# A hybrid recurrence block: 18 weight blocks keep their lower parts in DRAM, and dense steps change places

## The chip, the cores and the metric

The kernel runs on one core of a Trainium2 chip. The metric is the device time of one execution in microseconds. Three executions of the kernel before took 2312.27, 2316.17 and 2316.66 us; their median is 2316.17 us. A fourth execution was profiled; it took 2310.18 us itself, and all lines of the profile belong to it.

An engine has its own queue of instructions and works them off in order: TensorE (PE) multiplies matrices, VectorE (DVE), ScalarE (ACT) and GpSimd (POOL) work on elements, and SyncE (SP) issues the DMA transfers between DRAM and the on-chip memory.

## The reference

One residual block over 1024 tokens of width 1024, in float32. The input is normalised and modulated by a condition `c` (six segments of 1024 values, `mod`), and one projection `w_in` feeds two token mixers and two gates:

```python
mod = (cond @ w_ada[l] + b_ada[l])[:, None, :]
u = layer_norm(x) * (1.0 + sc1) + sh1
proj = u @ w_in
q, f, i, g, z, xbc, dt, gate_a, gate_b = jnp.split(proj, offs, axis=-1)
y_a = hgrn2_mixer(q, f, i, g, lb, gnorm) @ w_branch_a
y_b = mamba2_mixer(z, xbc, dt, conv_w, conv_b, dt_bias, a_log, d_skip, ssm_norm) @ w_branch_b
merged = jax.nn.sigmoid(gate_a) * y_a + jax.nn.sigmoid(gate_b) * y_b
x = layer_norm(ALPHA * x + g1 * (merged @ w_o), ln1_g[l], ln1_b[l])
u = layer_norm(x) * (1.0 + sc2) + sh2
x = layer_norm(ALPHA * x + g2 * swiglu(u, ...), ln2_g[l], ln2_b[l])
```

The first mixer (HGRN2) has 8 heads, each a gated linear recurrence with a 128 x 128 state. The second (Mamba-2) has 4 groups of 8 heads; its inputs x, B and C pass a causal convolution of four taps and a silu, and its output is gated by z and normalised per group. Both are computed in chunks over the tokens.

## The kernel before, in words

**Products.** A float32 product is made of three matmuls in a rounded format: each operand is split into an upper part (a cast) and a lower part (operand minus upper part), and lower x upper, upper x lower and upper x upper are added in PSUM (`Dense.mm`, L81 to L83). A weight block is 128 x 1024 (512 KB). `Dense.load` (L65 to L77) loads it into a buffer `raw`, casts it on ACT into `wh` (L75), and subtracts on the engine `dn.lo` to get `wl` (L76). There are two buffers each for `raw`, `wh` and `wl`. `Dense.unit` multiplies one block with both halves of 512 tokens: 8 steps of 3 matmuls for each half, and after each half a function evacuates the PSUM bank.

**Stages.** In time order:

1. 0 to 361 us: modulation, then products that are formed in pairs of blocks with fewer multiplications (gate A, g, z). Among the first pairs stand halves of plain gate blocks.
2. 361 to 467 us, the `i` stage (L558 to L594): the projection `i` and dt, three groups of 352 columns (`iwh`, `iwl`, four raw pieces `iraw` for each group, which use the `raw` buffers too), eight row tiles each. A row tile is 24 matmuls of 352 columns, evacuated on ACT into `i_sb` (L587). Beside it `mods`, a generator, loads blocks `wa` of `w_ada` and adds them up on DVE (L217), for the modulation segments that are needed later; it is advanced after each row tile. `step_sizes` computes Mamba's decays.
3. 467 to about 790 us, `hgrn_phase`: dense units for f and q of each head (lower parts on POOL), with the score, output and state products of the chunks between them.
4. About 790 to 1263 us, `mamba_phase`: dense units for B, C and four x blocks of each group (`dense_x`), followed by the rest of gate B; between them the chunks of the groups (transposes `trx` L871, scores `cb`, `yx` L910, `yi` L918). Lower parts are made on POOL here too.
5. To 1500 us the branch maps (`dqs`), to 1680 us the output projection and norm, then the FFN.

**What sets the order.** In stages 3 and 4 the dense units hang in one chain of generators, `Fill`, and `fill.to(n)` advances it until n steps are done. A step is three matmuls of 512 columns. `HF0` is the number of steps ahead of the first head's preparation, `HF1` the number ahead of its first scores; `share(i)` gives the steps done by chunk i. In mamba, `96 + LEAD` steps stand ahead of the first chunk, 12 go with each chunk of the first three groups, and what is left of `total` is spread over the last group's eight chunks; `LATE` steps remain behind them. `NGB` is the number of gate B blocks done before mamba. A scheduling layer then fixes the order of each engine's queue within these bounds. All transfers are issued by SP, in one order.

Of the kernel before, what the change touches and what calls it, by code (L numbers as in the profile page):

```python
# [9 lines left out]
F32 = mybir.dt.float32  # L10
# [3 lines left out]
ALU = mybir.AluOpType  # L14
PSUM = bass.MemoryType.PSUM

HF0, HF1 = 40, 52
F0, F1 = 0, 3
LATE, LEAD = 32, 12
NGB = 2  # L20
NE0, XJ = 1, 3
NG = 8
IE, MO = "VVVV", 4
# [9 lines left out]
P = 128  # L33
T = 1024
TT = T // P
# [3 lines left out]
HA = 8  # L39
# [11 lines left out]

B_Q, B_F, B_G, B_Z, B_X, B_B, B_C, B_GA, B_GB = 0, 8, 16, 24, 40, 56, 60, 64, 72
NBLK = 80

C_CT, C_BADA, C_CW, C_CB, C_DS, C_NW, C_GN, C_LB = 0, 8, 56, 152, 176, 192, 208, 209
NCOL = 225
# [4 lines left out]
class Dense:  # L61
# [2 lines left out]
    def __init__(self, tc, pool, psum):  # L64
        self.nc, self.pool, self.psum, self.lo = tc.nc, pool, psum, tc.nc.vector  # L65

    def load(self, src, scale=None, into=None, eng=None):
        nc = self.nc
        raw = self.pool.tile([P, 1024], F32, tag="raw", name="raw")
        nc.sync.dma_start(out=raw, in_=src)  # L70
        if scale is not None:
            r2 = raw.rearrange("p (k n) -> p k n", k=2)
            nc.vector.tensor_tensor(r2, r2, scale[:, None, :].broadcast_to([P, 2, TH]), op=ALU.mult)
        wh, wl = into or [self.pool.tile([P, 1024], F32R, tag=t, name=t) for t in ("wh", "wl")]
        nc.scalar.copy(wh, raw)  # L75
        (eng or self.lo).tensor_tensor(wl, raw, wh.bitcast(F32), op=ALU.subtract)  # L76
        return wh, wl  # L77

# [4 lines left out]
        nc.tensor.matmul(ps, sh, mh, start=False, stop=last)  # L83

    def unit(self, src, uh, ul, evac, ths=(0, 1), fine=False):
        wh, wl = src if isinstance(src, (tuple, list)) else self.load(src)
        wh = wh.rearrange("p (k n) -> p k n", k=KT)
        wl = wl.rearrange("p (k n) -> p k n", k=KT)
        for th in ths:
            ps = self.psum.tile([P, TH], F32, tag="d", name="dps")  # L90
            for kt in range(KT):
                self.mm(ps, wh[:, kt, :], wl[:, kt, :], uh[th][:, kt, :], ul[th][:, kt, :],
                        kt == 0, kt == KT - 1)
                if fine and kt < KT - 1:
                    yield
            evac(th, ps)
            yield
# [18 lines left out]
def chain(*gens):  # L116
    for g in gens:
        yield from g
# [3 lines left out]
def hybrid_block(ctx, tc, x, w_mod, w_ada, w_blk, w_i, w_ba, w_bb, w_o, w_g, w_u, w_d,  # L122
                 cols, masks, rows, hrows, out):
    nc = tc.nc
# [25 lines left out]
    z_d = tc.dram_tile([16, P, T], F32, name="z_d")  # L150
    h_d = tc.dram_tile([NFT, P, T], F32, name="h_d")
    x1_d = tc.dram_tile([TT, P, D], F32, name="x1_d")

    mk = const.tile([P, NMASK, P], F32, name="mk")
    cl = const.tile([P, NCOL], F32, name="cl")
# [84 lines left out]
    def gate_evac(which, n, logs=False):  # L240
        dst = (ga_d, gb_d)[which]

        def evac(th, ps):
            sg = wp.tile([P, TH], F32, tag="ge", name="ge")
            if logs:
                act(sg, ps, AF.Exp, scale=-1.0)
                act(sg, sg, AF.Ln, bias=ones[:, 0:1])
                act(sg, sg, AF.Exp, scale=-1.0)
            else:
                act(sg, ps, AF.Sigmoid)  # L250
            nc.sync.dma_start(out=dst[n, :, TH * th:TH * th + TH], in_=sg)
        return evac

    def gate_units(which, n0, n1, fine=False, ths=(0, 1)):
        for n in range(n0, n1):
            yield from dn.unit(w_blk[(B_GA, B_GB)[which] + n], uh, ul, gate_evac(which, n, fine), ths, fine=fine)
# [16 lines left out]
    with tc.tile_pool(name="sw", bufs=1) as sw, tc.tile_pool(name="s0p", bufs=2, space=PSUM) as pp:  # L273
# [149 lines left out]
        for k in range(4):  # L423
            modulate(1, k)
            modulate(1, 4 + k)
            u0, u1 = xT[1][:, k, :], xT[1][:, 4 + k, :]
            c = wp.tile([P, TH], F32, tag="ge", name="ge")
            V.tensor_tensor(c, u1, u0, op=ALU.subtract)
            split(t3[0][:, k, :], t3[1][:, k, :], c, V)
            V.tensor_tensor(u0, u0, b11[0][:, k, :].bitcast(F32), op=ALU.subtract)  # L430
            V.tensor_tensor(u0, u0, b11[1][:, k, :].bitcast(F32), op=ALU.subtract)
            split(t1[0][:, k, :], t1[1][:, k, :], u0, V)
            V.tensor_tensor(u1, u1, u0, op=ALU.subtract)
            split(t2[0][:, k, :], t2[1][:, k, :], u1, V)
            V.tensor_tensor(u0, b21[0][:, k, :].bitcast(F32), u1, op=ALU.subtract)
            V.tensor_tensor(u0, u0, b21[1][:, k, :].bitcast(F32), op=ALU.add)
            split(t4[0][:, k, :], t4[1][:, k, :], u0, V)
            if ns < NF:
                early(ns, *load_a(pairs[ns][0]))
                ns += 1  # L440
            if k % 2:
                n = 6 + k // 2
                for _ in dn.unit(dn.load(w_blk[B_GA + n]), uh, ul, gate_evac(0, n), (0,)):
                    pass
        while ns < NF:
            early(ns, *load_a(pairs[ns][0]))
            ns += 1
# [108 lines left out]
    with tc.tile_pool(name="s1", bufs=2, reuse_waits="tile") as sp, \  # L556
# [6 lines left out]
        def load_i(g, k4):  # L563
            raw = wp.tile([P, 1024], F32, tag="raw", name="iraw")[:, 0:2 * NI].rearrange("p (k n) -> p k n", k=2)
            nc.sync.dma_start(out=raw, in_=w_i[g, :, 2 * k4:2 * k4 + 2, :])
            return raw

        bridge = dn.load(w_blk[B_GA + 6])
        iraw = [load_i(0, k4) for k4 in range(2)]
        for g in range(3):  # L570
            wh = sp.tile([P, KT, NI], F32R, tag="iwh", name="iwh")
            wl = sp.tile([P, KT, NI], F32R, tag="iwl", name="iwl")
            for k4 in range(4):
                ks = slice(2 * k4, 2 * k4 + 2)
                raw = iraw.pop(0) if iraw else load_i(g, k4)
                split(wh[:, ks, :], wl[:, ks, :], raw, V if IE[k4] == "V" else G)
            if g == 0:
                for _ in dn.unit(bridge, uh, ul, gate_evac(0, 6), (1,)):
                    pass
                lower_bound()  # L580
            for tt in range(TT):
                ps = psd.tile([P, TH], F32, tag="d", name="dps")
                th, o = tt // 4, P * (tt % 4)
                for kt in range(KT):
                    dn.mm(ps[:, 0:NI], uh[th][:, kt, o:o + P], ul[th][:, kt, o:o + P], wh[:, kt, :], wl[:, kt, :],
                          kt == 0, kt == KT - 1)
                S.copy(i_sb[:, tt, NI * g:NI * g + NI], ps[:, 0:NI])  # L587
                mods.to((TT * g + tt + 1 - MO) * 36 / (24 - MO))
                if g == 1 and tt == 4:
                    steps.drain()  # L590
            if g == 0:
                steps = Fill(step_sizes(sp, pp))
                steps.to(1)
        mods.drain()  # L594


    def hgrn_phase():
        with tc.tile_pool(name="h", bufs=2, reuse_waits="tile") as hp, \
# [162 lines left out]
                nc.sync.dma_start(out=ya_d[h, :, TH * hf:TH * hf + TH], in_=y)  # L761

            units = [dense_fq(h) for h in range(HA)]
            fill = Fill(chain(*units, gate_units(0, 7, 8, True, (1,)), gate_units(1, 0, NGB, True)))
            fill.to(HF0)
            for g in (prep(0), arrays(0, 0)):
                for _ in g:
                    pass
            fill.to(HF1)
            score(0, 0)  # L770
            total = 16 * (2 * HA + NGB) + 8

            def share(i):

# [31 lines left out]
    def mamba_phase():  # L806
        with tc.tile_pool(name="m", bufs=2, reuse_waits="tile") as mp, \
# [3 lines left out]
            def dense_x(g):  # L811
# [6 lines left out]
                for blk, dst in [(16 + g, bT), (20 + g, cT)] + [(4 * g + j, xT[:, j, :]) for j in range(4)]:  # L818
# [22 lines left out]
                                act(t, t, AF.Silu, bias=cl[:, C_CB + k:C_CB + k + 1])  # L841
                            held[:] = held[1:] if len(held) == 2 and not th else []

                    yield from dn.unit(w_blk[B_X + blk], uh, ul, evac, fine=True)

            def fetch(g, ch):

# [620 lines left out]
```

## Time and profile before

| | |
|---|---|
| median of three runs | 2316.17 us |
| profiled execution, its own time | 2310.18 us |
| its span in the trace | 2308.4 us |
| TensorE busy | 2230.2 us, 97% |
| VectorE, ScalarE, GpSimd busy | 1567.8, 1061.6, 264.8 us |
| mean DMA rate over the span | 126 GB/s |

The trace names instructions by line and tile. A wait is listed with the instruction that released it, and a window gives each engine's busy time, the clock that TensorE was granted as a share of full speed, the share of time that the 16 DMA engines were busy, and the rate that they moved. A gap on TensorE costs time; a gap on another engine does only if something waits for it.

### The profile page before, as it was taken

The page shows a single profiled execution, that of the slowest core. Times are in us where ns is not written, and L with a number is a line of the kernel's source. Part 1 is how long each engine was busy: PE and PEld are TensorE (multiplying, and loading weights), DVE is VectorE, ACT ScalarE, POOL GpSimd, SP SyncE. Part 2 cuts the span into 40 slices and gives each one's busy share as a digit, 9 for nine tenths or more (in the row PEclk, how much of TensorE's full clock was granted, in tenths as well). Part 3 has the DMA queues.
Part 4 walks back from the last instruction along what each step waited for, and adds up shares of the span by engine and source line. Part 5 has one row for each costly group of instructions (what it writes and reads, how often), then busy time and mean ns, then how long its engine had stood idle before and what let it go on. Part 6 is the DMA issues. An engine that isn't in the chain of part 4 may idle for free.

```text
span 2308.4 us, 32125 instructions
## 1 busy us (share of the span) xinstructions
PE 2230.2 (97%) x12412; PEld 1816.2 (79%) x12412; DVE 1567.8 (68%) x2489; ACT 1061.6 (46%) x1931; POOL 264.8 (11%) x153
## 2 busy tenths in 40 slices
PE   7899999999999999999998999999899999999998
PEld 4778889977777787787776788888788888888886
DVE  5866665638898558898975443468977666653647
ACT  3833333137777646777786320224633333322221
POOL 0000000012222222222231000003400000000000
PEclk9999999999999999999999999999999999999999
DMA  7334326601112312343455643432232222244554
GB/s 282 121 140 136 126 93 209 218 33 52 61 56 69 118 61 92 110 141 115 159 164 183 229 167 102 132 138 95 73 132 101 87 73 92 73 160 151 179 182 132
DMA packets 119649, 290.75 MB, mean 126 GB/s; under 512 B 12101, under 2 KB 26949, under 8 KB 119497
## 3 DMA queue, kind: packets, MB, share of 16 engines
q1 hardware_dynamic: 119496, 288.71, 37.5%
q8 instruction: 97, 1.59, 0.3%
q14 instruction: 56, 0.45, 0.1%
HBM read 235.05 MB, written 53.62 MB: 125 GB/s over the span
## 4 chain that ended last, share of the span: by engine, by line
PE 82%; DVE 8%; ACT 3%; issue 3%; DMA 2%; POOL 2%; SPq 0%; DVEq 0%; POOLq 0%; ACTq 0%
PE dps L81 11%; PE dps L83 11%; PE dps L82 11%; PE fps L81 9%; PE fps L82 9%; PE fps L83 9%; PE dqs L81 4%; PE dqs L83 4%; PE dqs L82 4%; PE hps L83 1%; PE hps L81 1%; PE hps L82 1%; PE sc_ps L701 1%; DVE xTm L832 1%; PE yi L918 1%
## 5 line engine op out<-in xcount | busy, mean ns | idle before, releaser
L81 PE MATMUL dps<-uh,wl 128*128 128x512 f32 x800 | 331.7, 415 | 3.3 <-POOL wl L76 3.3
L83 PE MATMUL dps<-uh,wh 128*128 128x512 f32 x800 | 316.5, 396 | 0.0
L82 PE MATMUL dps<-ul,wh 128*128 128x512 f32 x800 | 314.8, 393 | 0.0
L76 POOL TENSOR_TENSOR wl<-raw,wh 128x1024 fp32r<-128x1024 f32 x49 | 132.1, 2696 | 790.4 <-ACT wh L75 723.4
L81 PEld LDWEIGHTS dps<-uh,wl 128*128 128x128 f32 x800 | 155.1, 194 | 37.6 <-issue 6.6
L83 PEld LDWEIGHTS dps<-uh,wh 128*128 128x128 f32 x800 | 151.9, 190 | 33.8
L82 PEld LDWEIGHTS dps<-ul,wh 128*128 128x128 f32 x800 | 152.5, 191 | 26.7
L81 PE MATMUL dqs<-yp,wl 128*128 128x512 f32 x384 | 147.5, 393 | 6.6 <-ACT yp L191 4.3
L82 PE MATMUL dqs<-yp,wh 128*128 128x512 f32 x384 | 150.4, 392 | 0.0
L83 PE MATMUL dqs<-yp,wh 128*128 128x512 f32 x384 | 150.1, 391 | 0.0
L179 POOL TENSOR_TENSOR mv<-mv,kc 128x1 f32<-128x1 f32 x32 | 32.3, 1015 | 1026.7 <-DVE mv L178 1023.5
L191 ACT CAST cw<-raw 128x512 fp32r<-128x512 f32 x131 | 81.0, 621 | 132.3 <-PE fps L83 87.6
L81 PE MATMUL fps<-t,cw 128*128 128x512 f32 x352 | 137.0, 389 | 0.7 <-DVE cw L192 0.7
L82 PE MATMUL fps<-t,cw 128*128 128x512 f32 x352 | 136.9, 389 | 0.0
L83 PE MATMUL fps<-t,cw 128*128 128x512 f32 x352 | 136.9, 389 | 0.0
L75 ACT CAST wh<-raw 128x1024 fp32r<-128x1024 f32 x76 | 79.6, 1048 | 113.5 <-PE dqs L83 101.8
L192 DVE TENSOR_TENSOR cw<-raw,cw 128x512 fp32r<-128x512 f32 x131 | 94.8, 725 | 43.5 <-ACT cw L191 42.2
L82 PE MATMUL fps<-wl,hp 128*128 128x512 f32 x304 | 118.4, 389 | 0.0
L83 PE MATMUL fps<-wh,hp 128*128 128x512 f32 x304 | 118.3, 389 | 0.0
L192 DVE TENSOR_TENSOR wl<-wdr,wh 128x1024 fp32r<-128x1024 f32 x38 | 46.5, 1224 | 105.4 <-ACT wh L191 105.2
L81 PE MATMUL fps<-wh,hp 128*128 128x512 f32 x304 | 117.0, 390 | 0.5 <-ACT wh L191 0.5
L191 ACT CAST wh<-wdr 128x1024 fp32r<-128x1024 f32 x38 | 40.1, 1054 | 147.4 <-PE fps L83 146.1
(368 smaller groups left out, 5586.4 us busy)
## 6 DMA issues: line engine op xcount, KB each, us to landing
raw<-in_w_blk_dram SPq DMA_DIRECT2D x79, 512.0 KB, 3.4
wdr<-in_w_d_dram SPq DMA_DIRECT2D x44, 512.0 KB, 3.8
wa<-in_w_ada_dram SPq DMA_DIRECT2D x32, 512.0 KB, 4.5
ac<-ac_d SPq DMA_DIRECT2D x32, 512.0 KB, 4.8
raw<-in_w_g_dram SPq DMA_DIRECT2D x26, 512.0 KB, 3.8
raw<-in_w_u_dram SPq DMA_DIRECT2D x26, 512.0 KB, 3.5
hr<-h_d SPq DMA_DIRECT2D x44, 256.0 KB, 3.9
h_d<-sg SPq DMA_DIRECT2D x18, 512.0 KB, 2.9
```

The source lines that it names most:

```text
L75: nc.scalar.copy(wh, raw)
L76: (eng or self.lo).tensor_tensor(wl, raw, wh.bitcast(F32), op=ALU.subtract)
L81: nc.tensor.matmul(ps, sl, mh, start=first, stop=False)
L82: nc.tensor.matmul(ps, sh, ml, start=False, stop=False)
L83: nc.tensor.matmul(ps, sh, mh, start=False, stop=last)
L179: G.tensor_tensor(mv[:, 2:3], mv[:, 1:2], kc[:, 2:3], op=ALU.pow)
L191: S.copy(hi, src)
L192: eng.tensor_tensor(lo, src, hi.bitcast(F32), op=ALU.subtract)
L701: PE.matmul(sp_[b0:b1, 0, b1:b2], lv[c][:, o + b0:o + b1], lv[c][:, o + b1:o + b2], start=True, stop=True)
L832: V.scalar_tensor_tensor(d[:, o:], ps[:, o + j - 3:TH + j - 3], cw(j), d[:, o:], op0=ALU.mult, op1=ALU.add)
L918: PE.matmul(yi[64 * e:64 * e + 64, j, :], xd[:, HP * hh:HP * hh + HP], ac[:, hh, :], start=True, stop=True)
```

## The change

It has three parts.

**Lower parts in DRAM.** The blocks of B, C and x of mamba's groups 1 to 3 (18 blocks, `AHEAD`) are loaded in the `i` stage, cast, subtracted on DVE, and the lower parts written to a DRAM tensor `wl_d`. This is a second generator, `make_lower`, which is advanced after each row tile beside `mods`. In mamba, these blocks are loaded and cast again, and their lower part is loaded from `wl_d` instead of being subtracted on POOL.

**Half gate blocks.** The first halves of gate B's blocks 0 and 1 move to the first pairs, next to the halves of gate A's blocks 6 and 7; their second halves, and all of block 2, are done in `hgrn_phase`, whose number of steps stays 296. The chain in mamba loses 16 steps.

**Counts.** HF0, HF1 go from 40, 52 to 32, 60; LEAD from 12 to 16. So the last group has 4 steps a chunk instead of 6.5, and the last 12 chunks of `hgrn_phase` have 2.33 instead of 3.

```diff
-HF0, HF1 = 40, 52
+HF0, HF1 = 32, 60
-LATE, LEAD = 32, 12
-NGB = 2
+LATE, LEAD = 32, 16
+NGB = 3
...
+AHEAD = [b for g in range(1, 4) for b in [B_B + g, B_C + g] + [B_X + 4 * g + j for j in range(4)]]
...
-    def load(self, src, scale=None, into=None, eng=None):
+    def load(self, src, scale=None, into=None, eng=None, lower=None):
...
         nc.scalar.copy(wh, raw)
+        if lower is not None:
+            nc.sync.dma_start(out=wl.bitcast(F32), in_=lower)
+            return wh, wl
         (eng or self.lo).tensor_tensor(wl, raw, wh.bitcast(F32), op=ALU.subtract)
...
-        wh, wl = src if isinstance(src, (tuple, list)) else self.load(src)
+        wh, wl = src() if callable(src) else src if isinstance(src, (tuple, list)) else self.load(src)
...
+    wl_d = tc.dram_tile([len(AHEAD), P, 1024], F32, name="wl_d")
...
+    made = {}
+    def weights(blk):
+        return (lambda: dn.load(w_blk[blk], lower=wl_d[made[blk]])) if blk in made else w_blk[blk]
+    def make_lower(blks):
+        last = None
+        for blk in blks + [None]:
+            wl = dn.load(w_blk[blk])[1] if blk is not None else None
+            if last:
+                made[last[0]] = len(made)
+                nc.sync.dma_start(out=wl_d[made[last[0]]], in_=last[1].bitcast(F32))
+            last = blk, wl
+            yield
...
             if k % 2:
-                n = 6 + k // 2
-                for _ in dn.unit(dn.load(w_blk[B_GA + n]), uh, ul, gate_evac(0, n), (0,)):
-                    pass
+                for which, n in ((0, 6 + k // 2), (1, k // 2)):
+                    for _ in gate_units(which, n, n + 1, ths=(0,)):
+                        pass
...
+        lower = Fill(make_lower(AHEAD))
...
                 mods.to((TT * g + tt + 1 - MO) * 36 / (24 - MO))
+                lower.to((TT * g + tt) * (len(AHEAD) + 1) / 22)
...
         mods.drain()
+        lower.drain()
...
-            fill = Fill(chain(*units, gate_units(0, 7, 8, True, (1,)), gate_units(1, 0, NGB, True)))
+            fill = Fill(chain(*units, gate_units(0, 7, 8, True, (1,)), gate_units(1, 0, 2, True, (1,)), gate_units(1, 2, NGB, True)))
...
-            total = 16 * (2 * HA + NGB) + 8
+            total = 16 * (2 * HA + NGB) - 8
...
-                    yield from dn.unit(w_blk[B_X + blk], uh, ul, evac, fine=True)
+                    yield from dn.unit(weights(B_X + blk), uh, ul, evac, fine=True)
```

The queues show what this does to the order. First ScalarE's queue in the `i` stage, from the third row tile of group 0 on in the kernel before (`i_sb` is a row tile's evacuation, `iwh` a cast of the next group's weights):

```order
L587 COPY i_sb<-dps 128x352 x3
L191 CAST iwh<-iraw 128x704
L587 COPY i_sb<-dps 128x352
L191 CAST iwh<-iraw 128x704
L587 COPY i_sb<-dps 128x352
L191 CAST iwh<-iraw 128x704 x2
```

and from the fourth row tile on in the changed one (`wh` is the cast of one of the 18 blocks):

```order
L610 COPY i_sb<-dps 128x352
L76 CAST wh<-raw 128x1024
L610 COPY i_sb<-dps 128x352 x2
L76 CAST wh<-raw 128x1024 x2
L610 COPY i_sb<-dps 128x352 x2
L76 CAST wh<-raw 128x1024
L141 ACTIVATE adt<-adt 128x256
L141 ACTIVATE hr<-hr 128x32
L196 CAST iwh<-iraw 128x704 x4
```

The four casts of group 1's weights stood between the third and the sixth evacuation; now all four stand behind the eighth, the seventh block's cast and two activations of `step_sizes`.

SP's queue at the same place, before, from the loads that follow group 0's last raw pieces:

```order
L213 DMA wa<-in_w_ada_dram 128x1024
L251 DMA ga_d<-ge 128x512
L213 DMA wa<-in_w_ada_dram 128x1024 x2
L516 DMA hr<-in_hrows_dram 128x64
L213 DMA wa<-in_w_ada_dram 128x1024 x4
L565 DMA iraw<-in_w_i_dram 128x704 x2
```

and now, the end of the same piece (`raw` are the 18 blocks, `wl_d` their lower parts on the way out):

```order
L272 DMA wl_d<-wl 128x1024
L218 DMA wa<-in_w_ada_dram 128x1024
L71 DMA raw<-in_w_blk_dram 128x1024
L272 DMA wl_d<-wl 128x1024
L538 DMA hr<-in_hrows_dram 128x64
L587 DMA iraw<-in_w_i_dram 128x704
L218 DMA wa<-in_w_ada_dram 128x1024
L587 DMA iraw<-in_w_i_dram 128x704
```

Group 1's first piece stood behind seven `wa` loads; now seven blocks and six written lower parts stand ahead of it as well.

Last, ScalarE's queue at the start of `hgrn_phase`, before (`ab<-dps` are evacuations of head 0's f, q and of the next head's f; `ab<-ab,mk` is the first instruction of head 0's preparation):

```order
L137 ACTIVATE ab<-dps 128x512 x2
L75 CAST wh<-raw 128x1024
L137 ACTIVATE ab<-dps 128x512
L617 COPY xq<-dps 128x512
L137 ACTIVATE ab<-dps 128x512
L617 COPY xq<-dps 128x512
L75 CAST wh<-raw 128x1024
L137 ACTIVATE ab<-dps 128x512
L137 ACTIVATE ab<-ab,mk 128x1024
```

and now:

```order
L141 ACTIVATE ab<-dps 128x512 x2
L76 CAST wh<-raw 128x1024
L141 ACTIVATE ab<-dps 128x512
L642 COPY xq<-dps 128x512
L141 ACTIVATE ab<-dps 128x512
L642 COPY xq<-dps 128x512
L141 ACTIVATE ab<-ab,mk 128x1024
L76 CAST wh<-raw 128x1024
```

The preparation stood behind the fifth evacuation; now it follows the fourth.

## The prediction

> **What bounds the kernel now.** I read the page's first two parts, the stretches of the `i` projection, and then what TensorE waited for in the later phases.
>
> ```profile
> span 2308.4 us, 32125 instructions
> PE 2230.2 (97%) x12412; PEld 1816.2 (79%) x12412; DVE 1567.8 (68%) x2489; ACT 1061.6 (46%) x1931; POOL 264.8 (11%) x153
> 1800.00:1900.00 100.00, 100.00 (x443) 82.81 (x442) 65.26 (x102) 31.80 (x53) 0.00 (x0) 1.00 0.23 79
> ```
>
> TensorE (PE) is busy for 97% of the span, so a matmul that moves without closing a gap changes nothing, and about 78 us of gaps (2308.4 − 2230.2), with the slower clock behind them, are all there is to win. The third row is a stretch of 100 us full of 512-column matmuls: 443 of them, 225.7 ns each. That is my price for a dense matmul; a dense *step* is three of them, 0.677 us.
>
> The stage in which the change adds most is the `i` projection, between about 361 and 467 us. The columns are: window, its length, busy time and count of PE, weight load, DVE, ACT and POOL, granted clock, DMA share, GB/s.
>
> ```profile
> 360.00:380.00 20.00, 19.89 (x121) 19.33 (x120) 13.50 (x20) 7.22 (x12) 0.00 (x0) 1.00 0.95 331
> 420.00:440.00 20.00, 20.00 (x133) 20.00 (x132) 10.50 (x11) 1.81 (x4) 0.00 (x0) 1.00 0.80 271
> 440.00:460.00 20.00, 20.00 (x119) 18.23 (x119) 11.02 (x10) 2.27 (x5) 0.00 (x0) 1.00 0.54 181
> DMA packets 7073, 22.51 MB, mean 212 GB/s; under 512 B 909, under 2 KB 1165, under 8 KB 7066
> iraw<-in_w_i_dram SPq DMA_DIRECT2D x8, 352.0 KB, 3.9
> raw<-in_w_blk_dram SPq DMA_DIRECT2D x4, 512.0 KB, 4.3
> ```
>
> PE waits for nothing here, ACT is nearly idle, DVE is half busy; the DMA engines are the resource closest to full, at 0.54 to 0.95 of their time. The last three rows are the transfers of 361 to 467 us: 22.51 MB in all, and a weight piece lands about 4 us after its issue.
>
> **The change part by part.**
>
> *Half gates among the pairs.* Two half blocks of gate B, 24 matmuls each, move there: 48 × 225.7 ns = **+10.8**. TensorE has no idle time in this stretch that they could fill (its two gaps of 4 us each are chains that start at a product standing behind them), so all of it is paid here and taken off in the last mamba group.
>
> *Eighteen lower parts made in the `i` stage.* Each adds a load, a cast on ACT, a subtraction on DVE and a write, in a stage whose durations are these:
>
> ```profile
> L217 DVE SCALAR_TENSOR_TENSOR acc<-wa,cond,acc 128x1024 f32<-128x1024 f32 x28 | 38.1, 1359 | 11.6 <-DMA wa<-in_w_ada_dram 11.4
> L192 DVE TENSOR_TENSOR iwl<-iraw,iwh 128x704 fp32r<-128x704 f32 x10 | 8.8, 889 | 7.5 <-ACT iwh L191 7.5
> L191 ACT CAST iwh<-iraw 128x704 fp32r<-128x704 f32 x9 | 7.0, 784 | 7.6 <-DMA iraw<-in_w_i_dram 7.6
> L76 POOL TENSOR_TENSOR wl<-raw,wh 128x1024 fp32r<-128x1024 f32 x2 | 5.2, 2608 | 350.1 <-ACT wh L75 350.1
> 461.40 0.45 ACT L587 COPY i_sb<-dps 128x352 f32<-128x352 f32 x1 [3.36 <-PE dps L83]
> 465.22 0.45 ACT L587 COPY i_sb<-dps 128x352 f32<-128x352 f32 x1 [3.36 <-PE dps L83]
> 1263.90 1.04 ACT L75 CAST wh<-raw 128x1024 fp32r<-128x1024 f32 x1
> 1264.96 1.23 DVE L76 TENSOR_TENSOR wl<-raw,wh 128x1024 fp32r<-128x1024 f32 x1 [6.12 <-ACT wh L75]
> ```
>
> ACT gains 18 × 1.04 = 19 us and DVE 18 × 1.23 = 22 us, which both have room for. What they have no room for is their place in the queues. The order (front part) shows the casts of the next group's weights, `iwh`, before the last row tiles of group 0 in the kernel before, and behind all eight copies, a `wh` cast and two small activations in the changed one. SP's queue stands likewise: the four pieces `iraw` come after seven blocks, six writes and seven `wa` loads, and every piece shares the two `raw` buffers with the blocks. Let 0 be the end of group 0's matmuls. Copy 0.45, cast 1.04 and subtraction 1.23 end at 2.7; only then is the buffer free that the second piece is loaded into. It lands at 6.6 (3.9 after its issue), is cast and subtracted (0.78 + 0.89) by 8.3, and frees the buffer of the fourth piece, which lands at 12.2 and is ready at 13.9. TensorE's order mixes three row tiles, so it works meanwhile; but some 26 of their 72 matmuls stand behind the first that needs the fourth piece. One tile of 24 takes 465.22 − 461.40 = 3.82 us, so the three are done at 13.9 + 4.1 = 18.0 instead of 11.5: 6.5 us late. The same order stands between groups 1 and 2. With 1 us each for the clock that drops after a wait (priced at the mamba rows below), that is 2 × 7.5 = 15. At the end, F0's raw block, which in the kernel before is loaded long ahead, now stands behind the last writes and loads; group 2 has some 24 transfers of about 1.6 us (0.52 MB at 331 GB/s), 38 us, against 8 × 3.82 + 6.5 = 37.1 us of matmuls and wait, and then cast 1.04 and POOL's 2.61 follow: about 5 us late. Sum **+20**. A second way to it: 22.51 MB and 36 transfers of 0.524 MB are 41.4 MB, which at the 331 GB/s of the full window take 125 us instead of the 106 there are: +19. Lower bound 0 (every load lands early and PE never waits; nothing waits now, so there is no gain); upper bound +34, if the volume's 19 and one boundary's wait come on top of each other with casts that hold up the copies, and so PSUM, in group 0 as well.
>
> The Trainium skill (DMA: Bandwidth & Descriptors, "Specifications" and "Bandwidth") puts the ceiling of the DMA fabric at 435 GB/s and measures about 425 GB/s for one core alone with 16 MB. By that, the 41.4 MB would take 97 us, the stage would not be bound by volume, and only the waits at the boundaries would be left of this term. The trace has half-microsecond slices above 400 GB/s between 360 and 380 us, but the mean there is 331 GB/s at a share of 0.95, and I keep the row.
>
> *Start of the recurrence.* Here the rows are:
>
> ```profile
> PE sc_ps L701 <- DVE e L676: 3.3, 1, 3.3
> PE sc_ps L705 <- DVE e L676: 3.2, 1, 3.2
> 510.00:520.00 10.00, 10.00 (x80) 6.94 (x79) 7.17 (x14) 6.07 (x15) 0.00 (x0) 0.74 0.01 2
> 489.01 0.60 ACT L137 ACTIVATE ab<-dps 128x512 f32<-128x512 f32 x1 [4.36 <-PE dps L83]
> 494.45 0.60 ACT L137 ACTIVATE ab<-dps 128x512 f32<-128x512 f32 x1 [3.42 <-PE dps L83]
> 494.94 1.14 ACT L137 ACTIVATE ab<-ab,mk 128x1024 f32<-128x1024 f32 x1
> 502.90 3.42 DVE L649 TENSOR_TENSOR ab<-b,ab 128x1024 f32<-128x1024 f32 x1
> ```
>
> PE waits 3.3 us at 505 and 3.2 at 544, and runs at 0.74 for 10 us after the first (2.6 lost). With HF0 at 32 the preparation of head 0 starts behind the evacuation at 489.0 and the copy, not behind that of 494.45: about 4.8 us earlier, less one cast (1.04) that now stands inside its chain. The subtraction on POOL that slows L649 to 3.42 falls elsewhere. But 168 dense matmuls stand before the first score in both orders, and in the new one all 16 score matmuls of a tile come at once, which need the last of the preparation. I expect the first wait to stay near 3, the second and half the lost clock to go: 3.2 + 1.3 + about 1.5 of clock after the second, **−6**. Bounds: −11 (both waits, the 2.6, and as much again after the second) and +4 (a full wait for the later part of the chain in place of 6 matmuls between). The last twelve chunks of this phase lose 8 dense matmuls of cover in all (2.33 steps a chunk, not 3, made up elsewhere): **+1**.
>
> *Mamba groups 0 to 2.*
>
> ```profile
> PE dps L81 <- POOL wl L76: 2.4, 1, 2.4
> PE dps L81 <- POOL wl L76: 1.0, 1, 1.0
> PE trx L871 <- ACT xTm L137: 4.0, 1, 4.0
> PE trx L871 <- ACT xTm L137: 3.4, 1, 3.4
> 1050.00:1060.00 10.00, 8.65 (x48) 7.26 (x49) 7.49 (x16) 7.60 (x18) 0.02 (x1) 0.83 0.39 107
> 1150.00:1160.00 10.00, 7.21 (x32) 5.91 (x32) 7.96 (x17) 6.90 (x18) 1.27 (x1) 0.83 0.39 130
> ```
>
> The first two waits are for lower parts from POOL, which these groups no longer make: −3.4. The two at the start of a group are for the last silu; LEAD 16 puts 4 more steps, 2.7 us, ahead of the transposes: −5.4. Behind each of the two stands a window at 0.83, some 1.4 us of clock (0.17 × 8.65), most of which goes: −2.2. Sum **−11**, bounds −14 (all four waits and both clocks) and −5 (the silus come late as before, behind casts that are still on ACT, and only the lower parts are won).
>
> *Last group and its end.*
>
> ```profile
> 1163.30:1213.30 50.00, 50.00 (x315) 38.76 (x314) 39.58 (x58) 42.71 (x103) 19.35 (x10) 1.00 0.59 184
> PE dqs L81 <- ACT yp L191: 4.3, 1, 4.3
> PE yi L918 <- ACT csh L191: 3.2, 1, 3.2
> ```
>
> 16 steps fewer are 48 × 225.7 ns, −10.8, if they are all on the path. A chunk keeps 4 dense steps of 6.5, so PE's part of its 8.3 us falls by 1.7 to 6.6; but DVE works 39.58/50 and ACT 42.71/50 of that, 6.6 and 7.1 us a chunk, of which ACT gives up only the gate activations that left. I take 7.05 a chunk: 8 × (8.35 − 7.05) = −10.4 of the −13.5 of these chunks; LEAD's 12 matmuls are paid ahead, +2.7. Behind the last sum stand 27 dense matmuls, not 42, so the wait for `yp` (4.3 now) grows by 15 × 0.2257 = 3.4. Sum −10.4 + 2.7 + 3.4 = **−4**, bounds −10.8 and +2 (chunks stay near 8).
>
> **Sum:** 10.8 + 20 − 6 + 1 − 11 − 4 = +10.8. The profiled execution took 2310.18 us, so it becomes 2321; the median of the three runs shown stands 6.0 above it, at 2316.17, and becomes **2327**.
>
> **Rivals.** (a) *The `i` stage absorbs its new work.* Its term is 0, the rest stays: −9.2, **2307**, faster. For it speak the idle ACT and DVE and a mean of 212 GB/s; the rate of the skill's page points the same way. Against it, the casts behind the eighth copy, an order that no early load can mend. (b) *DMA and SP's order decide the whole stage.* Each late block holds up ACT's copies and so PE already in group 0; the term is +34 and the sum +25, **2341**, slower. It decides from the point where 41.4 MB do not fit into the stage and its waits, 106 + 14 us, at under 345 GB/s; 331 speaks for it, against it that early pieces overlap. (c) *The waits removed are worth their upper bounds*: −11 at the recurrence, −14 and −10.8 in mamba, the rest standing: 10.8 + 20 − 11 + 1 − 14 − 10.8 = −4, **2312**, no change that can be told. For it, the clock rows show that a wait costs more than its length; against it, the busy DVE and ACT of the last group.
>
> **How the numbers follow.** A run of this kernel can be told from no change by about 0.2%, 4.6 us. My forecast gets 0.48, (b) 0.15, (a) 0.19, (c) 0.18. The forecast's own spread, ±7, lies nearly all above 2320.8. Slower 0.61, within 0.2% 0.18, faster 0.21. The range runs from 2304, a little under (a), to 2342, at (b); all low ends together (2292) and all high ones (2363) are outside.
>
> **What would show it.** In the new profile: PE gaps of some 6 us in all near the 8th and 16th row tile of the `i` stage, released by `iwl` or `iwh`, and one before F0 released by `wl` of POOL or the load; about 41 MB in that stage and its length near 126 us. No `wl` of POOL in groups 1 to 3, waits for `xTm` under 1.5 us. Last-group chunks of 7 us and a wait for `yp` of 7 to 8 us. An `i` stage of about 106 us would make the prediction wrong on its largest term, chunks at 6.6 or 8 us on the last.

## The result, and the profile after

The changed kernel takes 2339.17 us (median of four runs, 2333.9 to 2342.39), the kernel before 2316.24 us beside it (median of four). The ratio is 1.0101, with a 95% interval of 1.0076 to 1.0126: slower by 0.8 to 1.3%. The profiled execution took 2333.9 us, against 2310.18 before.

The page's lines of the changed kernel:

```profile
span 2332.1 us, 32262 instructions
PE 2234.4 (96%) x12412; PEld 1818.4 (78%) x12412; DVE 1566.9 (67%) x2509; ACT 1087.3 (47%) x1953; POOL 218.3 (9%) x135
```

And four stretches of it: the `i` stage up to F0's first matmul, the recurrence up to mamba's first transpose, mamba up to group 3's first transpose, and the last group with its end. Columns as in the prediction.

```profile
372.00:505.00 133.00, 111.37 (x638) 103.25 (x636) 80.53 (x94) 41.75 (x61) 2.38 (x2) 0.91 0.86 303
505.00:914.00 409.00, 391.15 (x3585) 311.00 (x3585) 285.48 (x561) 266.36 (x525) 92.85 (x41) 1.00 0.21 70
914.00:1187.50 273.50, 273.50 (x1573) 217.85 (x1572) 234.93 (x420) 220.45 (x460) 29.33 (x21) 1.00 0.50 161
1187.50:1291.60 104.10, 88.26 (x515) 68.53 (x513) 80.61 (x113) 80.30 (x176) 23.38 (x12) 0.96 0.56 177
```

TensorE does the same work in a longer span. In the `i` stage it is busy for 111 of 133 us, in the recurrence it idles for 18 us (8 before), and in mamba's first three groups it no longer waits at all. With the same boundaries in both traces (first matmul of the `i` stage, first dense matmul of F0, first `trx`, first `trx` of group 3, first `dqs`), the 23.7 us between the spans divide like this:

| stretch, us | before | after | difference | prediction |
|---|---|---|---|---|
| start to `i` stage | 361.6 | 372.1 | +10.5 | +10.8 |
| `i` stage to F0 | 105.4 | 132.9 | +27.5 | +20 |
| F0 to first transpose | 397.0 | 409.0 | +12.0 | −2.3 (−6 + 1, and LEAD's 2.7) |
| to group 3's first transpose | 284.9 | 273.5 | −11.4 | −7.2 (−11 without the 3.8 for group 3's silu wait and its clock) |
| last group and end, to `dqs` | 118.8 | 104.1 | −14.7 | −10.5 (−4 without LEAD's 2.7, and those 3.8) |
| `dqs` to the end | 1040.8 | 1040.5 | −0.3 | 0 |

The second of the two silu waits in the prediction, 3.4 us, ends at 1152.8 us, behind group 3's first transpose; so 2.7 + 1.1 of the −11 belong to the last row but one.

The waits of TensorE in the `i` stage (engine, line and tile that waited, who released it; us in all, times, longest):

```profile
PE dps L85 <- ACT iwh L196: 10.4, 2, 6.9
PE mps L236 <- DVE acc L222: 6.9, 1, 6.9
PE mps L227 <- DVE acc L222: 2.6, 1, 2.6
PE dps L86 <- DVE iwl L197: 1.7, 3, 0.8
```

The same view of the recurrence, between 545 and 795 us:

```profile
PE sc_ps L730 <- DVE eb L707: 7.5, 8, 1.5
PE sc_ps L730 <- ACT xq L642: 3.0, 5, 0.6
```

The first list is where the prediction put it: 10.4 us at the two group boundaries, for `iwh`. The end waits for `acc`, the modulation sum whose last `wa` arrives late, and not for F0's block. The second list was not foreseen: about 1 us for `eb` and 0.6 for `xq`, once in most heads.

In the `i` stage TensorE's idle time grew from 2.2 to 21.6 us. The other 8 us are the same matmuls taking longer, 111.3 us and not 103.1, at a mean granted clock of 0.91, where it was 1.00. The lowest ten microseconds stand behind the first boundary wait:

```profile
411.00:421.00 10.00, 7.89 (x30) 7.43 (x31) 9.47 (x16) 2.76 (x5) 0.00 (x0) 0.58 0.96 319
```

### The profile page after: what moved, and what is told of

It reads as the page before. It is cut to its first block, busy times and chain, and to the rows that moved or that the text cites. A ratio compares the mean times of both kernels' runs of the same rounds, so it can differ in the third digit from the quotient of the medians.

```text
span 2332.1 us, 32262 instructions
## 1 busy us (share of the span) xinstructions
PE 2234.4 (96%) x12412; PEld 1818.4 (78%) x12412; DVE 1566.9 (67%) x2509; ACT 1087.3 (47%) x1953; POOL 218.3 (9%) x135
## 5 line engine op out<-in xcount | busy, mean ns | idle before, releaser
L76 ACT CAST wh<-raw 128x1024 fp32r<-128x1024 f32 x96 | 100.5, 1047 | 129.7 <-PE dqs L87 102.4
L80 POOL TENSOR_TENSOR wl<-raw,wh 128x1024 fp32r<-128x1024 f32 x31 | 79.9, 2579 | 751.7 <-DMA raw<-in_w_blk_dram 439.5
L197 DVE TENSOR_TENSOR wl<-wdr,wh 128x1024 fp32r<-128x1024 f32 x38 | 46.5, 1224 | 105.4 <-ACT wh L196 105.2
```

The costliest lines, as they stand in the source:

```text
L197: eng.tensor_tensor(lo, src, hi.bitcast(F32), op=ALU.subtract)
```

## The experiments

Each ratio is taken against the kernel before, run beside that kernel; its median lay between 2316.2 and 2319.7 us. The stretches of every run, by the same boundaries (us, from one profiled execution each):

| run | start | `i` stage | recurrence | groups 0 to 2 | last group | `dqs` to end |
|---|---|---|---|---|---|---|
| before | 361.6 | 105.4 | 397.0 | 284.9 | 118.8 | 1040.8 |
| changed | 372.1 | 132.9 | 409.0 | 273.5 | 104.1 | 1040.5 |
| no_lower | 372.8 | 109.7 | 411.6 | 293.2 | 110.9 | 1040.3 |
| early_split | 372.1 | 135.4 | 412.9 | 273.5 | 103.6 | 1040.7 |
| no_traffic | 373.7 | 118.6 | 410.2 | 293.1 | 110.3 | 1040.5 |
| hf_back | 370.7 | 135.4 | 399.7 | 273.5 | 103.5 | 1041.9 |
| hf1_alone | 364.4 | 109.5 | 405.8 | 284.7 | 117.8 | 1043.3 |
| lead_alone | 361.7 | 108.8 | 402.7 | 293.9 | 117.1 | 1043.1 |
| twelve | 370.9 | 116.9 | 401.8 | 279.2 | 107.7 | 1041.4 |
| six_hf0 | 373.1 | 104.7 | 395.1 | 289.6 | 106.0 | 1041.5 |
| six_lead12 | 370.7 | 104.7 | 393.9 | 285.5 | 107.3 | 1042.7 |
| six_plain | 360.9 | 107.8 | 394.8 | 283.1 | 116.0 | 1042.9 |
| hf0_alone | 360.6 | 109.6 | 393.0 | 284.3 | 118.6 | 1045.3 |
| pool_writes | 361.1 | 129.9 | 393.5 | 275.4 | 116.7 | 1042.2 |

Two to four microseconds of difference between two runs in a stretch are not to be read: the same program part took 105.4, 108.8 and 109.6 us in the `i` stage of three runs.

**1. The changed kernel without the lower parts in DRAM (no_lower).** `AHEAD` is empty and mamba subtracts on POOL.

```diff
-AHEAD = [b for g in range(1, 4) for b in [B_B + g, B_C + g] + [B_X + 4 * g + j for j in range(4)]]
+AHEAD = []
...
```

> The changed kernel without its first part: no block is made ahead, mamba subtracts on POOL again; half gates and counts stay as changed. Theory: the i stage alone pays for this part. Between its first matmul and F0 the changed kernel took 132.9 us (372.1 to 505.0), the kernel before 105.3; here it should take 105 to 106, a gain of 27. The waits for POOL's lower parts in mamba come back, 3.4. So about 2339 - 27 + 3 = 2315, level with the kernel before (2316). Rival: part of the i stage's growth comes from the half gates or the shifted start and stays; then 2325 or more.

Measured: 2340.89 us, ratio 1.0093 (1.0071 to 1.0115). The `i` stage went back to 109.7, as expected, and the kernel is still as slow. What it wins there it loses in mamba: 293.2 + 110.9 against 273.5 + 104.1, 26.5 us. So the first part of the change pays for itself in the changed kernel, and my price for it in mamba, the two waits of 3.4 us in all, was far too low. POOL's subtractions and three DVE groups in groups 0 to 2, by line, in this run (POOL's row is from the same view of that engine):

```profile
L80 POOL TENSOR_TENSOR wl<-raw,wh 128x1024 fp32r<-128x1024 f32 x17 | 45.0, 2645 | 156.3 <-ACT wh L76 109.2 <-PE cb L895 14.8 <-PE trx L893 14.4
L857 DVE SCALAR_TENSOR_TENSOR xTm<-edge,cl,xTm 128x3 f32<-128x3 f32 x33 | 17.8, 539 | 0.0
L948 DVE TENSOR_TENSOR Sm<-Sm,eal 128x512 f32<-128x512 f32 x18 | 19.5, 1086 | 0.2
L854 DVE SCALAR_TENSOR_TENSOR xTm<-dps,cl,xTm 128x509 f32<-128x509 f32 x45 | 33.3, 740 | 0.1
```

and in the changed kernel:

```profile
L80 POOL TENSOR_TENSOR wl<-raw,wh 128x1024 fp32r<-128x1024 f32 x1 | 2.4, 2398 | 13.7 <-ACT wh L76 13.7
L860 DVE SCALAR_TENSOR_TENSOR xTm<-edge,cl,xTm 128x3 f32<-128x3 f32 x33 | 11.1, 335 | 0.0
L951 DVE TENSOR_TENSOR Sm<-Sm,eal 128x512 f32<-128x512 f32 x18 | 12.7, 708 | 0.2
L857 DVE SCALAR_TENSOR_TENSOR xTm<-dps,cl,xTm 128x509 f32<-128x509 f32 x45 | 33.2, 739 | 0.1
```

With 17 subtractions of 2.6 us on POOL in this stretch, the same DVE instructions take 539 and 1086 ns in the mean, with one of them 335 and 708. Single ones take up to 1.9 and 2.9 us. The third group, which reads one input from PSUM (`dps`), takes 740 and 739. The two groups that grow have all their inputs in SBUF, the on-chip memory that POOL reads. The Trainium skill (SBUF — State Buffer, "Who interferes with whom") says that a DVE instruction with two such inputs and a GpSimd instruction that reads the memory exclude each other for their whole length; the rows agree, down to an update of 3 elements that takes half a microsecond in the mean. DVE is busy for 251 us of these groups here and for 235 in the changed kernel. TensorE's waits here come to 12.6 us, none of them for POOL; the other 7 us are matmuls at a mean clock of 0.98 (busy 280.3 us, 273.5 in the changed kernel). That DVE's slower instructions make these waits is read from the rows; no run left the subtractions out alone.

**2. The next group's pieces earlier (early_split).** The four `iraw` pieces are loaded, cast and subtracted after row tiles 0 to 3 of the group ahead.

```diff
...
                 S.copy(i_sb[:, tt, NI * g:NI * g + NI], ps[:, 0:NI])
+                if g < 2 and tt < 4:
+                    piece(parts, g + 1, tt)
                 mods.to((TT * g + tt + 1 - MO) * 36 / (24 - MO))
```

> The changed kernel with one edit: the four pieces of the next group's i weights are loaded, cast and subtracted after the first four row tiles of the group ahead, before the block of that tile, not after its last tile. Same transfers, casts and subtractions, same 40 MB. Theory (order): the waits at the two group boundaries, 3.5 + 0.8 and 6.9 us with the clock behind them, go; the wait of 2.7 for the modulation sum and the end of the stage (6.9 and F0 late) stay or grow somewhat. i stage 132.9 - 13 = 120, total 2326. Rival (volume): 40 MB at 331 GB/s need 122 us and start some 9 us into it, wherever the pieces stand; what is won at the boundaries is lost at the end, i stage 130 to 133, total 2337 to 2339.

Measured: 2341.5 us, ratio 1.01 (1.0074 to 1.0127); `i` stage 135.4. TensorE's waits in it:

```profile
PE mps L236 <- DVE acc L222: 22.9, 1, 22.9
PE mps L227 <- DVE acc L222: 3.5, 1, 3.5
PE dps L86 <- DVE iwl L197: 0.3, 1, 0.3
```

The boundary waits are gone, and all that they cost stands at the end, in one wait of 22.9 us. The rival, volume, fits, 2 us above its range in the stage and in the total: the boundaries were a place where the debt was paid, and not its cause.

**3. The lower parts made but not moved (no_traffic).** The 18 writes and 18 later loads are dropped, POOL subtracts in mamba.

```diff
-                nc.sync.dma_start(out=wl_d[made[last[0]]], in_=last[1].bitcast(F32))
...
-        return (lambda: dn.load(w_blk[blk], lower=wl_d[made[blk]])) if blk in made else w_blk[blk]
+        return w_blk[blk]
```

> The changed kernel whose 18 blocks are still loaded, cast and subtracted on DVE in the i stage, but whose lower parts are not written, and are not loaded in mamba, which subtracts on POOL again. This takes 18 writes (9.4 MB) out of the i stage: some 31 MB stay. Volume theory: 31 MB at 331 GB/s are 94 us, less than the 105 there are, so the i stage is back at 105 to 109. Order theory: the four casts of the third group's weights still stand behind the eighth copy and the raw buffers are still shared; one boundary wait of 5 to 7 us and the late last loads stay, i stage 115 to 122. Total 2339 - (11 to 27) + 3 for the POOL waits: 2331 by order, 2316 by volume.

Measured: 2347.83 us, ratio 1.0119 (1.0096 to 1.0142); `i` stage 118.6, with 10.5 us of wait, 5.9 of it for `iwh` in four pieces. That is within the order theory's range and above the volume theory's: without the writes, the loads, casts and shared buffers still cost 9 us (no_lower took 109.7), and the writes' share is 132.9 − 118.6 = 14. The total was missed by 17, since mamba's groups went to 293.1 + 110.3, for the reason found in run 1.

**4. HF0 and HF1 as before (hf_back).**

```diff
-HF0, HF1 = 32, 60
+HF0, HF1 = 40, 52
```

> The changed kernel with HF0, HF1 = 40, 52 as before. In the changed kernel the recurrence, from F0 to the first transpose of mamba, took 409.0 us, against 397.0 before, of which LEAD is 2.7; new in it are waits of 1.0 and 0.6 us for eb (DVE) and xq (ACT) once in each head, and 3.3 and 2.6 at its end. Theory: HF1 = 60 shifts the dense units against the chunks by 8 steps, so that a dense evacuation falls on the chunk whose eb is needed: with 52 the waits go, the recurrence takes 399 to 401, total 2329 to 2331. Rival: the waits come from the third gate block and the fewer steps of the last twelve chunks, or from the late start; then they stay, 407 to 409, total 2338.

Measured: 2328.22 us, ratio 1.0047 (1.0032 to 1.0062); recurrence 399.7, which is 397.0 and LEAD's 2.7. The waits for `eb` and `xq` are gone. The two counts alone carry all of the recurrence's loss, and some 11 us of the 23.

**5. HF1 alone (hf1_alone)**, on the kernel before.

```diff
-HF0, HF1 = 40, 52
+HF0, HF1 = 40, 60
```

> The kernel before with one number changed, HF1 from 52 to 60 (HF0 stays 40). Theory: HF1 alone brings the waits of the recurrence, since it sets which chunk the scans and evacuations of the next head fall on: F0 to the first transpose grows from 397 to 406 or more, with waits of about 1.0 us for eb (DVE) and 0.6 for xq in each head, and the profiled time is about 2310 + 10 = 2320. Rival: it takes HF0 = 32 (an earlier preparation) or the third gate block; then 396 to 399 and about 2310.

One execution took 2327.28 us; recurrence 405.8, 8.8 more, and the waits are there:

```profile
PE sc_ps L705 <- DVE eb L682: 6.7, 7, 1.1
PE sc_ps L705 <- ACT xq L617: 3.0, 5, 0.6
```

It is HF1. What it moves is seen at one head in the timelines of the kernel before (start, length, engine, instruction, count):

```profile
593.70 3.69 DVE L638 TENSOR_TENSOR_SCAN b<-mk,b 128x128 f32<-128x128 f32 x8 [0.46 <-ACT b L137]
594.99 1.49 POOL L760 TENSOR_TENSOR y<-y,sq 128x512 f32<-128x512 f32 x1 [8.76 <-ACT sq L137]
597.31 0.66 DVE L682 TENSOR_TENSOR eb<-eb,xq 128x512 f32<-128x512 f32 x1
599.52 0.20 PE L705 MATMUL sc_ps<-eb 128*32 128x32 f32 x1
```

and of the changed one:

```profile
593.34 5.84 DVE L663 TENSOR_TENSOR_SCAN b<-mk,b 128x128 f32<-128x128 f32 x8 [0.46 <-ACT b L141]
594.95 2.58 POOL L80 TENSOR_TENSOR wl<-raw,wh 128x1024 fp32r<-128x1024 f32 x1 [14.79 <-ACT wh L76]
597.49 1.41 POOL L785 TENSOR_TENSOR y<-y,sq 128x512 f32<-128x512 f32 x1
599.11 0.60 DVE L736 COPY_PREDICATED sc<-mk,sc_ps 128x128 f32<-128x128 uint32 x2
599.61 0.68 DVE L707 TENSOR_TENSOR eb<-eb,xq 128x512 f32<-128x512 f32 x1
600.35 0.27 PE L730 MATMUL sc_ps<-eb 128*32 128x32 f32 x8 [0.98 <-DVE eb L707]
```

In both, eight scans for the next head's preparation stand in DVE's queue ahead of the product `eb` that the current scores need. Before, they take 3.7 us, beside one POOL instruction of 1.5 us, and `eb` is ready 1.6 us before its matmuls start. With 8 more dense steps ahead, which is two chunks at 4 steps each, POOL's subtraction for a dense block falls on the scans. They take 5.8 us, the longest single one 2.5 and the usual one 0.4, and `eb` comes 1 us too late. hf1_alone has the same at six heads (5.84 us for eight scans); in hf_back they take 3.7 again. By these rows the cause is the one of run 1, DVE held up by POOL. No run took this subtraction off POOL, and the waits for `xq` were not followed up.

**6. HF0 alone (hf0_alone)**, on the kernel before: `HF0, HF1 = 32, 52`.

> The kernel before with HF0 = 32 alone (HF1 stays 52). In the run with 6 blocks the recurrence took 395.1 with LEAD 16, 2.7 of it for LEAD: 392.4 against 397.0 before. If HF0 does this, as the prediction's term for the start had it, F0 to the first transpose is 392 to 393 here and the total 2316.7 - 4.6 = 2312. If it came with the third gate block and the half steps, 397 and no difference.

Measured: 2312.18 us, ratio 0.9972 (0.9961 to 0.9983): faster. The recurrence took 393.0; its waits between 500 and 765 us are

```profile
PE sc_ps L701 <- DVE e L676: 3.0, 1, 3.0
PE sc_ps L705 <- DVE eb L682: 0.9, 4, 0.2
PE sc_ps L705 <- DVE e L676: 0.5, 1, 0.5
```

The first wait stays at 3.0 and the second, 3.2 at 544 us, is gone (the 0.5 stands at 756 us, where the kernel before has 0.3), as the prediction's term for the start had it (−6; measured −4.0). One such difference could be chance; but the five runs with HF0, HF1 = 32, 52 took 392.4 to 394.8, LEAD's 2.7 taken off, and the four with 40, 52 took 397.0 to 400.0. In the changed kernel HF1 covered the gain up.

**7. LEAD alone (lead_alone)**, on the kernel before: `LATE, LEAD = 32, 16`.

> The kernel before with LEAD 16 instead of 12. The prediction gave this count 7.6 us of gain by the waits for the silu of xT (4.0 and 3.4 us). By it, first transpose to group 3's first takes 285.0 - 7 = 278, the recurrence 2.7 more, the last group 2.7 less of work: total 2309. Rival, from the run without lower parts made ahead, where these groups took 293.2: with POOL still subtracting, 4 more steps ahead only move POOL's and DVE's work to other places, DVE stays the bound of these groups, and they take 285 to 293: total 2316 to 2322.

Measured: 2328.93 us, ratio 1.0047 (1.0031 to 1.0062): slower. Groups 0 to 2 took 293.9, 9 more than with LEAD 12:

```profile
PE dps L81 <- DVE cT L835: 4.0, 2, 2.7
PE cb L873 <- ACT bt L892: 3.4, 3, 1.7
PE trx L871 <- DVE kx L890: 3.1, 1, 3.1
PE dps L81 <- DVE xTm L832: 2.4, 2, 1.4
```

The silu wait of 4.0 us is gone from this list, and the one of 3.4, behind its end, is down to 0.4. So the prediction's term did what it said, and yet the waits come to 13.8 us where the kernel before has 8.8, most of them released by DVE, and the busy time rose from 276.2 to 280.0. DVE was no busier (249 of 294 us; 255 of 285 before), so that it bounds these groups is not shown, and why four steps ahead cost 9 us stays open. Run 1 fits: the 293 us there are LEAD 16 with POOL still subtracting. With the lower parts in DRAM the count costs nothing: 275.4 with LEAD 12 (run 12) and 273.5 with 16.

**8. Twelve blocks (twelve).** Groups 2 and 3 alone, the pieces early, HF0, HF1 = 40, 52.

```diff
-HF0, HF1 = 32, 60
+HF0, HF1 = 40, 52
...
-AHEAD = [b for g in range(1, 4) for b in ...]
+AHEAD = [b for g in range(2, 4) for b in ...]
```

> The changed kernel with HF0, HF1 = 40, 52, the next group's i pieces after the first four row tiles, and lower parts made ahead for the 12 blocks of groups 2 and 3 alone: 35 MB in the i stage in place of 40 or 41. Theory (volume, and POOL's cost in mamba by the block): 35 MB at the 303 to 331 GB/s seen take 106 to 116 us, so the i stage takes 108 to 118 instead of 135; first transpose to group 3 takes 277 to 281 (one group of three keeps POOL), the rest as with the old counts: 2328 - 22 + 5 = 2311, faster than the kernel before by 5 or more. Rival: the i stage's cost is not the volume but the wait on single late loads, and stays at 125 or more: 2320 to 2326.

Measured: 2320.4 us, ratio 1.0009 (0.9993 to 1.0024): no difference from the kernel before. The `i` stage took 116.9, within the volume theory's 108 to 118; the groups 279.2, as expected. The total is 9 above the one expected: against hf_back the `i` stage gave 18.5 and not 22, and the last group (107.7 for 103.5) and the recurrence took 6 more.

**9. Six blocks with HF0 = 32 (six_hf0).** Group 3 alone, the pieces early, `HF0, HF1 = 32, 52`.

> As the run with 12 blocks, but with 6 (group 3 alone: 29 MB in the i stage) and HF0, HF1 = 32, 52. By volume the i stage takes 106 to 109. First transpose to group 3 takes 283 to 289, since two of three groups keep POOL and LEAD is 16. If HF1 makes the waits of the recurrence, F0 to the first transpose is 395 to 399 (397 + 2.7 for LEAD, less 2 to 4 of the first wait); if HF0 does, 405 to 409. Total 2310 to 2316 by the first, 2320 and more by the second.

Measured: 2314.31 us, ratio 0.9982 (0.9969 to 0.9994): a little faster than the kernel before. The `i` stage took 104.7 with 28.7 MB, and the recurrence 395.1, so the six blocks cost nothing there. The DMA row of the `i` stage, in the run with all 18 blocks, early_split:

```profile
DMA packets 11914, 40.23 MB, mean 297 GB/s; under 512 B 1443, under 2 KB 1699, under 8 KB 11906
```

in that with twelve:

```profile
DMA packets 10186, 33.94 MB, mean 290 GB/s; under 512 B 1251, under 2 KB 1507, under 8 KB 10178
```

and in this one:

```profile
DMA packets 8754, 28.72 MB, mean 274 GB/s; under 512 B 1091, under 2 KB 1347, under 8 KB 8746
```

In these three, with the pieces early, the stage took 135.4, 116.9 and 104.7 us. At 290 to 300 GB/s its own 105 us hold some 31 MB, an estimate from these rows; the bytes above that are paid in time, and 28.7 MB were free. No run with early pieces stood at 31; no_traffic moved 30.8 MB with the pieces late and took 118.6, so the volume alone does not give that run's length.

**10. The same with LEAD 12 (six_lead12).**

> The run with 6 blocks and HF0, HF1 = 32, 52, with LEAD back at 12. By the run with LEAD alone, 4 steps of LEAD cost the groups that keep POOL about 9 us. Here two of three groups keep it: first transpose to group 3 goes from 289.6 to 281 to 284, the recurrence loses the 2.7 of the steps, the last group gains them: total about 2314 - 7 = 2307. If LEAD matters only together with all 18 blocks on POOL, nothing changes: 2314.

Measured: 2310.66 us, ratio 0.9973 (0.9962 to 0.9984); groups 285.5 instead of 289.6. The medians of the two runs differ by 3.7 us, about half of what was expected, and their intervals overlap.

**11. Six blocks, no half gates (six_plain).** As run 10, with `NGB = 2` and the pairs as in the kernel before, so that HF0, six lower parts and the early pieces of run 2 are what differs from it.

> The same without the half gates among the pairs and with NGB 2, as before; what is left of the change is the lower parts of group 3's 6 blocks, and HF0 = 32. The half gates cost 10.5 to 11 us ahead of the i stage. If the last group's shortening (118.8 before, 104 to 106 with them) comes from the 16 steps that they take away, it goes back by as much: last group 115 to 117 and the same total as the run beside this one, within 2 us. If it comes from the lower parts of group 3, which DVE and POOL no longer make there, it stays near 108 and the total is 8 us lower, near 2299.

Measured: 2306.5 us, ratio 0.995 (0.9938 to 0.9962): faster than both kernels, by 0.4 to 0.6% than the one before. HF0 alone had 2312.18 beside the same runs of that kernel (run 6), so six lower parts with early pieces bring another 5.7 us. Against run 10, the start became 9.8 us shorter in the profiles and the last group 8.7 longer: the half gates only move work, and 1 us is within the spread of stretches. The medians say 4 us for leaving them out; that they cost as much is not shown by the stretches.

**12. All 18 blocks, writes from POOL's queue (pool_writes).** As run 11, with

```diff
-AHEAD = [b for g in range(3, 4) for b in ...]
+AHEAD = [b for g in range(1, 4) for b in ...]
...
-                nc.sync.dma_start(out=wl_d[made[last[0]]], in_=last[1].bitcast(F32))
+                nc.gpsimd.dma_start(out=wl_d[made[last[0]]], in_=last[1].bitcast(F32))
```

> The run with HF0 = 32 and no other count changed (LEAD 12, NGB 2, no half gates), but with all 18 blocks made ahead, and the 18 writes of lower parts issued from POOL's queue, which does nothing in the i stage, not from SP's, where they waited 36 to 40 us for DVE in front of the loads. Theory 1: SP's order held the loads up; freed, 40 MB go at 340 GB/s and more, the i stage takes 115 to 120. Theory 2: the DMA engines give about 300 GB/s for this mix of reads and writes whatever the queue; then 130 to 136. The groups of mamba take 273 to 275, the last group 110 to 116. Total by theory 1 about 361 + 118 + 395 + 274 + 113 + 1042 = 2303 in the profile, by theory 2 2319.

Measured: 2321.14 us, ratio 1.0007 (0.9997 to 1.0016); `i` stage 129.9, with this DMA row:

```profile
DMA packets 11923, 40.26 MB, mean 307 GB/s; under 512 B 1445, under 2 KB 1701, under 8 KB 11915
```

and these waits of TensorE:

```profile
PE mps L236 <- DVE acc L222: 11.5, 2, 8.0
PE dtps L561 <- issue: 9.2, 1, 9.2
```

Theory 2: with SP's queue free of the writes, the transfers go at 307 GB/s, not at 340. Who issues them decides little (135.4 us and 297 GB/s in early_split). The gap of 9.2 us hides nothing of it, since the stage still ends with a wait of 8.0 for `acc`. That the DMA engines stood at 0.85 to 0.88 of their time and not at 1 is not explained: SP's loads waited here for DVE's subtractions and sums (17.0 and 15.3 us in all), since `raw` has two buffers and `wa` three, and more buffers, which would tell, were not tried.

## Why the prediction was right or wrong

The direction and the range held; the size did not: +22.9 us in the medians against +10.8 forecast, 2339 in 2304 to 2342. Step by step:

*Half gates, +10.8.* Right: +10.5. By run 11 the last group gives back about as much, and no more.

*`i` stage, +20.* The step that failed is the sum of two boundary waits and a late F0. Of its two ways, the second (41.4 MB at 331 GB/s against the stage's 106 us) had the mechanism, and the first only the place. The boundary waits came at 6.9 us each with what went with them, near the 6.5 worked out, but run 2 took them away and the stage stayed as long. The mis-sized number was the rate: 297 to 307 GB/s where it counts, not the 331 of one full window, so 132.9 us instead of 125. The idle time of this stage grew by 19.4 us, close to the 18 of the working, though its end waited for `acc` and not for F0's block; the clock behind the waits was given 2 us and took 8. The prediction also read that TensorE waits for nothing in this stage of the kernel before, where it idles for 2.2 us. Rival (b) named the volume and put the kernel at 2341. That the kernel came out near this is luck: (b) had +34 here, where +27.5 came, and left the recurrence at the forecast, which added 14, and mamba, which took off 8 more. The 425 GB/s of the Trainium skill (DMA: Bandwidth & Descriptors, "Bandwidth"), by which 41 MB would have been hidden, were not reached as a mean in any run of this stage; the row was the better guide and still too high.

*Start and end of the recurrence, −6 and +1.* Wrong by 14 us, and the largest error. HF0 did what was said (run 6: −4.0 in the stretch). The step that failed is that HF1 = 60 was taken as no more than the 168 matmuls ahead of the first score, which it left alone. The prediction had POOL's subtraction "falls elsewhere" and did not ask onto what: it falls on the scans of the later heads and makes them 2.2 us longer. The bound of +4 was for a single wait at the start, and the wait comes back in most heads (run 5).

*Groups 0 to 2, −11.* Of this, −7.2 belong to the stretch, which gave −11.4, and the working behind them is wrong. The lower parts were given 3.4 us, for the waits that name POOL; beside LEAD 12 they are worth 9.5 (284.9 against run 12's 275.4) and beside LEAD 16 they are worth 20 (run 1). LEAD was given 7.6 for both silu waits and their clock; it gives some 2 here beside the lower parts and costs 9 without them (run 7). So the two terms do not add, and that −11 and −11.4 look alike is luck. POOL's subtractions cost more through DVE than through the waits that name POOL. The window of these groups in the kernel before shows how little room DVE has, busy for 255 of 285 us:

```profile
863.90:1148.90 285.00, 276.20 (x1573) 218.78 (x1572) 255.15 (x418) 214.81 (x457) 70.59 (x36) 0.99 0.38 121
```

That a wait removed beside so full an engine comes out at another matmul is how run 7 reads; it is not shown to be the reason.

*Last group, −4.* Too small by 4 in its stretch (−14.7 against −10.5). The lower parts, which had no term here, are worth 7 us beside the changed counts (110.9 without them, 104.1 with them), but only 2 to 3 beside the old ones (118.8 before, 116.7 and 116.0 in runs 12 and 11). From the second `trx` to the seventh a chunk takes 6.6 us (8.2 before), the value that the prediction named as a sign against its 7.05. The wait for `yp` grew by 1.0 (4.3 to 5.3), not by 3.4.

## What to carry to other kernels

Where an engine off the path makes the instructions of another one longer, count that time, and ask onto which of them it falls after a shift; the waits that name it are only a part (here 3.4 us of 9 to 20). A stage with idle DMA engines has room for only so many megabytes at the rate its own rows sustain; divide first, and move only that much (here six of 18 blocks). And a count that shifts one stream against another is judged at every place where the streams meet, not only at the first.

## What the runs showed of the hardware that I had not expected

A gap of TensorE before the first `dtps` matmul in the `i` stage, for which the profile names no releaser ("issue"), took 2.09 us in the kernel before, 3.74 and 4.22 in two other runs of the same program part, and 9.19 in pool_writes:

```profile
424.88 1.19 PE L561 MATMUL dtps<-adt,mk 128*128 128x256 f32 x2 [9.19 <-issue]
```

The DMA engines were fullest in pool_writes (0.88), but that does not explain it: the changed kernel, early_split and hf_back move the same 40 MB at a share of 0.85 to 0.86 and have no such gap. Its cause is open. It is also part of why the `i` stage of the same program took 105.4 to 109.6 us.
